# Slots of matching offsets, one task for two blocks of dots, and a third conv pair behind the layer norm's mean

## The chip, the cores and the metric

The kernel runs on one core of one Trainium2 chip. The metric is the time of one execution on the device in microseconds (us), as a median over runs. The engines are named as in the profile: PE is TensorE, DVE is VectorE, ACT is ScalarE, POOL is GpSimd, SP is SyncE, which here only issues DMAs.

## What is computed

Two residual layers on one sequence of 1024 tokens with 1024 channels, in float32. Each layer has a token mixer and a gated feed-forward part, each behind a root-mean-square norm whose result is shifted and scaled by vectors that come from a conditioning vector `c`. The stack ends with one more norm.

```
c_act = silu(c)
for i in range(2):
    mod = c_act @ ada_w[i] + ada_b[i]
    sh_m, sc_m, g_m, sh_f, sc_f, g_f = split(mod, 6)
    h = rms_norm(x, norm_mix_g[i]) * (1 + sc_m) + sh_m
    if i == 0:      # convolution module
        a, g = split(h @ w1 + b1, 2)
        u = a * sigmoid(g)
        u = causal_depthwise_conv(u, w_dw, width=31) + b_dw
        y = silu(layer_norm(u, ln_g, ln_b)) @ w2 + b2
    else:           # pooling mixer
        y = pooled_differences(h) @ w_grp * ls
    x = x + (1 + g_m) * y
    h = rms_norm(x, norm_ffn_g[i]) * (1 + sc_f) + sh_f
    x = x + (1 + g_f) * ((silu(h @ w_gate) * (h @ w_up)) @ w_down)
return rms_norm(x, final_g)
```

## The kernel before, in words

**Layout.** Channels lie on the 128 partitions, so a tensor of 1024 channels is 8 tiles (`KT`), and the 2816 channels inside the feed-forward part are 22 tiles (`NF`). The tokens are cut into two chunks of 512, A (`ch.i == 0`) and B (`ch.i == 1`). A product therefore multiplies a 128x128 weight block with a 128x512 operand.

**Three products for one.** Each float32 operand is split into a high part and a low part in the type float32r, and `products` (L423) issues three matmuls: weight high with operand high, weight high with operand low, weight low with operand high. A weight tile is loaded as 512 KB through SP (`raw`); ACT copies the high part and its negative, and a DMA from POOL adds the tile once more to the negative, which leaves the low part (`load_weight`, L408). Up to five weight tiles are held ahead (`W_BUFS`).

**Where the operands lie.** `slot_after` (L243) draws tiles of `ch.n + 2 - 2 * ch.i` values: 514 values, 2056 bytes, in chunk A and 512 values, 2048 bytes, in chunk B. `slot` (L239) hands out the last 512 values of such a tile. In these slots lie the high and low parts of the normed input (`hhi`, `hlo`), of the conv module's last operand (`vhi`, `vlo`), of the pooled differences (`mxhi`, `mxlo`), and of the conv input for the taps that TensorE takes (`uhi`, `ulo`). A second kind, `wslot` (L247), is 542 values, 2168 bytes, wide, eight per chunk: the gated conv input `u` with 30 values of history ahead of it, the normed input `hp` of the pooling mixer, and the high and low parts of the feed-forward's inner values (`ghi`, `glo`, L900).

**The order of the work.** The program is a list of units (L547) that are emitted one after the other. TensorE's order is the order of emission. Beside the units there are tasks (`Task`, L210, and `Taps`, L660) that give small steps to VectorE, GpSimd and ScalarE. `pace` (L187) is called every few products and lets tasks step as long as an estimated clock of the engine is less than 4 us ahead of the estimated clock of TensorE. `finish` (L199) emits all that is left of a task, with no regard to pauses. A task can ask for a pause in estimated time (`LOAD`: "load" and "next" 4.0, "slow" 18.0, "dots" 3.5 us).

**The convolution stage.** `conv_in` (L601) computes one tile of `a` and one of `g` of a chunk, a pair of 24 matmuls each, and `conv_glu` gates them into `u`. The 31 taps of a tile of A are then a `Taps` task: each tap is one operation on VectorE (accumulator in PSUM) or, with a helper multiplication on ScalarE, one addition on GpSimd. Tile 7 of A is taken by TensorE with all 31 taps, and tile 6 with eight (`PE_TAPS`, L46), as products with diagonal matrices (`pe_taps`, L636); a tap that reaches back by an odd number of tokens reads its operand one value off. When the taps of all eight tiles are there, `layer_norm_silu` (L739) sums the tiles, TensorE spreads the mean, VectorE centres, ScalarE squares, and so on up to `vhi` and `vlo`. Then `conv_out` (L780) multiplies them with `w2`, 192 matmuls, and adds up the squares for the next norm.

The units stand in this order: pairs 4 and 5 of A; pairs 6 and 7 of A and then of B; pairs 0, 1, 2 of B; the tap units of tiles 6 and 7; then the taps of A are finished; pairs 3 and 4 of B (`HOLD_LN = 2`), in whose course the mean comes; `conv_out` of A; pair 5 of B with the norm of the feed-forward part of A (`norm_a`); then the feed-forward part of A, during which VectorE and GpSimd do the taps and the layer norm of B.

**The dots.** Most of `mod` is computed on VectorE: `ada_dot` (L315) multiplies a 128x1024 tile of `ada_w`, 512 KB, with `c_act` and sums it. A block of `mod` (one of the six parts `j`) takes eight dots. `ada_task` (L324) makes a task of them; its tiles go through two buffers (`ADA_BUFS`) that all such tasks share, loaded by SP. Blocks 4 (the scale of the feed-forward norm) and 5 (the gate behind it) of layer 0 are two tasks that are put up ahead of `conv_out` of A; behind `conv_out` the unit at L1147 finishes that of block 4. Block 4 is needed by `norm_a`, block 5 by the first down products. The 48 dots of layer 1 are one task, put up at the start of the feed-forward part of A with pauses of 18 us; `ada_need` (L1099) forces what is missing in the third unit of B's feed-forward part.

**The feed-forward parts.** For each chunk and layer: `ffn_p1` computes one tile of gate and up, 24 matmuls each, `ffn_p2` the down products of two such tiles, 48 matmuls, six for each of the eight output tiles. They follow in the order A layer 0, B layer 0, A layer 1, B layer 1, with the mixers of layer 1 between.

Of the kernel before, what the change touches and what calls it, by code (L numbers as in the profile page):

```python
# [16 lines left out]
P = 128  # L17
# [8 lines left out]
WINDOWS = (2, 4, 8, 16)  # L26
PHALO = max(WINDOWS) - 1
EPS = 1e-6

# [85 lines left out]
def trunk(ctx, tc, xT, c, vec, ada, adan, w1f, w1, wdg, w2, wgu, wdn, wpl, out):  # L115
# [123 lines left out]
    def slot(ch, name, dt=F32R):  # L239

        return slot_after(ch, name, dt)[:, 2 - 2 * ch.i :]

    def slot_after(ch, name, dt=F32R):  # L243

        return slots.tile([P, ch.n + 2 - 2 * ch.i], dt, tag=f"s{ch.i}", name=nm(name))

    def wslot(ch, name, dt=F32):  # L247

        return slots.tile([P, ch.width], dt, tag=f"u{ch.i}", name=nm(name), bufs=KT)

# [324 lines left out]
    def conv_u(ch, p):  # L575
        u = st["u", ch.i, p] = wslot(ch, "u")
        if ch.i == 0:
            G_.memset(u[:, :HALO], 0.0)
        else:
            G_.tensor_copy(u[:, :HALO], uhalo[:, p, :])  # L580
        return u

    def conv_glu(ch, p, ba, bg):
# [3 lines left out]
        if ch.i == 0 and PE_TAPS.get(p) == CW:  # L587

            V_.scalar_tensor_tensor(ba, ba, V("conv_b1", p), sg, op0=ADD, op1=MUL)
            hi, lo = st["us", p] = [slot_after(A, name) for name in ("uhi", "ulo")]  # L590
            for part in (hi, lo):
                G_.memset(part[:, :2].bitcast(F32), 0.0)
            S_.copy(hi[:, 2:], ba)
            V_.tensor_tensor(lo[:, 2:], ba, hi[:, 2:].bitcast(F32), op=SUB)
            S_.copy(uhalo[:, p, :], ba[:, ch.n - HALO :])
            return
# [4 lines left out]
    def conv_in(*todo):  # L601

        def emit(take):
            got = {}
            for each in todo:
# [14 lines left out]
                conv_glu(ch, p, *b)  # L620
                if ch.i == 0 and 0 < PE_TAPS.get(p, 0) < CW:
                    split_u(p)
                if ch.i == 0 and PE_TAPS.get(p, 0) < CW:
                    T["taps", 0, p] = Taps(A, p, PE_TAPS.get(p, 0))
        tiles = list(dict.fromkeys(e[1] for e in todo if e))
        unit(emit, *[w1[p, i] for p in tiles for i in range(2)])

    def split_u(p):


        u = st["u", 0, p][:, HALO - 2 :]
        hi, lo = st["us", p] = [slot_after(A, name) for name in ("uhi", "ulo")]
        S_.copy(hi, u)
        either(A.n).tensor_tensor(lo, u, hi.bitcast(F32), op=SUB)

    def pe_taps(p):  # L636

        groups = tap_groups(p)
        us = []
        for i, js in enumerate(groups):  # L640
            def emit(take, i=i, js=js):
# [3 lines left out]
                for q, j in enumerate(js):  # L645
                    o = (CW - 1 - j) // 2 * 2
                    i0 = 2 - (CW - 1 - j) % 2
                    products(b[:, o:], wt, q, [v[:, i0 : i0 + A.n - o] for v in st["us", p]], j == CW - 1, j == CW - PE_TAPS[p])
                    if q % 4 == 3:
                        pace()  # L650
                if i == len(groups) - 1:
                    if PE_TAPS[p] == CW:
                        S_.activation(st["u", 0, p][:, HALO:], b, AF.Identity, bias=V("conv_bdw", p))
# [6 lines left out]
    class Taps:  # L660
# [4 lines left out]

        def __init__(self, ch, p, others=0):
            self.ch, self.p, self.done, self.urgent = ch, p, False, False
            self.next, self.acc, self.part = 0, None, None

            self.end, self.awaits, self.other = CW - max(others, 1), others > 0, None  # L670
            tasks.append(self)

        def step(self, e):
# [4 lines left out]
            if self.done:  # L678
                return False
            if self.next < self.end:  # L680
                if e == "V" and self.acc is None and sum(isinstance(t, Taps) and t.acc is not None for t in tasks) >= 2:
                    return False
                if e == "G":
                    if self.acc is None and self.part is None and sum(isinstance(t, Taps) and t.part is not None for t in tasks) >= 2:
                        return False
                    if self.next >= self.end - 2:
                        return False
                j = self.next
                self.next += 1
                if e == "V":  # L690
# [18 lines left out]
            if e != "V" or self.awaits and self.other is None:  # L709
                return False  # L710
            d = u[:, HALO : HALO + n]
            if self.awaits:
                if self.part is not None:
                    V_.tensor_tensor(d, self.part, self.acc, op=ADD)
                else:
                    S_.copy(d, self.acc)
                V_.tensor_tensor(d, d, self.other, op=ADD)
            else:
                if self.part is not None:
                    V_.tensor_tensor(self.acc, self.part, self.acc, op=ADD)  # L720
                V_.scalar_tensor_tensor(d, d, w(CW - 1), self.acc, op0=MUL, op1=ADD)
            self.done = True
# [84 lines left out]
    def pool_h(ch, l):  # L807

        hp = st["hp", ch.i] = [wslot(ch, "hp") for _ in range(KT)]
        for k in range(KT):  # L810
# [62 lines left out]
    def ffn_p1(ch, l, f, pick, first):  # L873
        def emit(take):
# [385 lines left out]
```

## Time and profile before

| | us |
|---|---|
| runs, median of 3 | 1873.54 |
| lowest and highest | 1871.35, 1875.83 |
| the profiled execution | 1871.14 |
| its span, first to last instruction | 1869.4 |
| PE, DVE, ACT, POOL busy | 1826.0, 990.9, 968.0, 614.8 |

An execution of the profile has a start and an end of each instruction. A matmul of the profile lasts longer than the distance to the next one, since matmuls are pipelined; so the cost of a product is read from the time that a run of them takes, divided by their number. A row of the timeline has start and length in us, engine, line, operation, the tiles by name as out<-in, and in brackets the idle time of the engine before it and what ended that. Nearly all instructions have line 109 or 131, the helpers that issue them, so they are told apart by tile. The granted clock is 1.00 where TensorE runs at full speed and 0.50 where it is given half.

### The profile page before, as it was taken

The numbers are of one execution on the slowest core, as the hardware profiler recorded it, in microseconds if no ns is written. First come the engines' busy times: TensorE is split into PE (matmuls) and PEld (weight loads), VectorE is DVE, ScalarE is ACT, GpSimd is POOL, SyncE is SP. The second block draws the span as 40 slices with busy tenths as digits, with TensorE's granted clock in tenths as the row PEclk, the third lists the DMA queues.
The fourth block names the chain that finished last, engine by engine and source line by source line (L and its number), as shares of the span: only waits on it lengthen the run. The fifth ranks groups of instructions, "written<-read, shape, count | busy, mean of one in ns | idle before, by whom it ended". The sixth has DMA issues, their size and how long they took to land.

```text
span 1869.4 us, 21783 instructions
## 1 busy us (share of the span) xinstructions
PE 1826.0 (98%) x8085; PEld 1481.9 (79%) x8085; DVE 990.9 (53%) x1528; ACT 968.0 (52%) x1240; POOL 614.8 (33%) x662
## 2 busy tenths in 40 slices
PE   7999998999999999999999999999999999999997
PEld 5777776888888888877888888888888888888886
DVE  8899856988875235585622233734432233322225
ACT  3775665766656454454644445644534454444443
POOL 4587522877733211272111111511111111111111
PEclk9999998999999999999999999999999999999998
DMA  7958797888978987999887878778778879788782
GB/s 289 300 151 221 172 263 222 225 222 208 223 189 216 231 221 185 283 261 269 227 194 178 211 171 205 182 173 205 181 178 196 192 177 250 176 205 197 181 195 68
DMA packets 108285, 387.56 MB, mean 207 GB/s; under 512 B 11793, under 2 KB 13969, under 8 KB 108178
## 3 DMA queue, kind: packets, MB, share of 16 engines
q0 software_dynamic: 44208, 160.98, 47.2%
q1 hardware_dynamic: 62880, 224.13, 34.6%
q8 instruction: 64, 1.05, 0.2%
q10 hardware_dynamic: 1090, 1.05, 0.2%
q14 instruction: 43, 0.35, 0.1%
HBM read 381.92 MB, written 4.19 MB: 207 GB/s over the span
## 4 chain that ended last, share of the span: by engine, by line
PE 82%; DVE 10%; DMA 6%; issue 1%; ACT 1%; SPq 0%; POOL 0%; DVEq 0%
PE gate L131 24%; PE up L131 24%; PE dn L131 24%; DMA adaw<-in_ada_dram 5%; DVE ca L109 4%; PE y L131 4%; PE first L131 3%; DVE adaw L109 1%; DVE acc L109 1%; PE g L131 1%; PE a L131 1%; DVE x L109 1%; DVE t L109 1%; DMA adaw<-in_adan_dram 1%; DVE hlo L109 1%
## 5 line engine op out<-in xcount | busy, mean ns | idle before, releaser
L109 ACT CAST w<-raw 128x1024 fp32r<-128x1024 f32 x317 | 331.0, 1044 | 508.2 <-issue 303.8
L131 PE MATMUL gate<-hhi,w 128*128 128x512 f32 x1408 | 455.4, 393 | 2.3 <-DVE x L109 1.7
L131 PE MATMUL up<-hhi,w 128*128 128x512 f32 x1408 | 455.9, 393 | 0.0
L131 PE MATMUL dn<-ghi,w 128*128 128x512 f32 (+1 forms) x1440 | 445.7, 386 | 1.2 <-DMA w<-in_wdn_dram 1.2
L417 POOL DMA_DIRECT2D w<-in_wgu_dram x176 | 154.6, 878 | 779.0 <-ACT w L109 759.4
L109 ACT ACTIVATE w<-raw 128x1024 fp32r<-128x1024 f32 x307 | 323.9, 1055 | 0.0
L109 DVE SCALAR_TENSOR_TENSOR x<-dn,gains,x 128x512 f32<-128x512 f32 (+1 forms) x360 | 261.8, 735 | 115.8 <-PE dn L131 115.3
L109 DVE TENSOR_TENSOR t<-t,up 128x512 f32<-128x512 f32 x86 | 59.0, 686 | 495.0 <-PE up L131 474.8
L131 PEld LDWEIGHTS dn<-ghi,w 128*128 128x128 f32 x1440 | 267.9, 188 | 59.8 <-DMA w<-in_wdn_dram 1.6
L131 PEld LDWEIGHTS gate<-hhi,w 128*128 128x128 f32 x1408 | 264.8, 188 | 62.6 <-DVE x L109 2.5
L131 PEld LDWEIGHTS up<-hhi,w 128*128 128x128 f32 x1408 | 264.7, 188 | 59.2 <-DMA w<-in_wgu_dram 0.3
L131 PE MATMUL dn<-glo,w 128*128 128x512 f32 (+1 forms) x720 | 278.7, 387 | 0.0
L131 PE MATMUL gate<-hlo,w 128*128 128x512 f32 x704 | 276.7, 393 | 1.5 <-DVE hlo L109 1.5
L131 PE MATMUL up<-hlo,w 128*128 128x512 f32 x704 | 276.5, 393 | 0.0
L109 POOL TENSOR_TENSOR pa<-pa,pr 128x512 f32<-128x512 f32 x156 | 222.9, 1545 | 13.6 <-ACT pr L109 10.9
L109 DVE SCALAR_TENSOR_TENSOR ca<-u,vecs,ca 128x512 f32<-128x512 f32 x257 | 177.8, 745 | 0.5
L131 PEld LDWEIGHTS gate<-hlo,w 128*128 128x128 f32 x704 | 132.6, 188 | 31.5 <-DVE hlo L109 2.3
L131 PEld LDWEIGHTS dn<-glo,w 128*128 128x128 f32 x720 | 135.2, 188 | 28.1 <-issue 0.2
L131 PEld LDWEIGHTS up<-hlo,w 128*128 128x128 f32 x704 | 132.6, 188 | 29.2
L417 POOL DMA_DIRECT2D w<-in_wdn_dram x88 | 78.3, 890 | 228.4 <-ACT w L109 226.5
L109 DVE SCALAR_TENSOR_TENSOR adaw<-adaw,cact 128x1024 f32<-128x1024 f32 x80 | 118.9, 1488 | 65.1 <-DMA adaw<-in_ada_dram 65.0
L109 ACT ACTIVATE t<-gate 128x512 f32<-128x512 f32 x86 | 51.1, 594 | 157.4 <-PE gate L131 155.4
(145 smaller groups left out, 1776.7 us busy)
## 6 DMA issues: line engine op xcount, KB each, us to landing
raw<-in_wgu_dram SPq DMA_DIRECT2D x176, 512.0 KB, 7.5
w<-in_wgu_dram POOLq DMA_DIRECT2D x176, 512.0 KB, 8.1
raw<-in_wdn_dram SPq DMA_DIRECT2D x88, 512.0 KB, 5.3
w<-in_wdn_dram POOLq DMA_DIRECT2D x88, 512.0 KB, 9.4
adaw<-in_ada_dram SPq DMA_DIRECT2D x64, 512.0 KB, 7.6
raw<-in_w_dram SPq DMA_DIRECT2D x36, 512.0 KB, 6.4
w<-in_w_dram POOLq DMA_DIRECT2D x34, 512.0 KB, 8.5
adaw<-in_ada_dram SPq DMA_DIRECT2D x8, 1024.0 KB, 5.3
```

Of the source, the lines that this page charges most:

```text
L109: self.last = self.order(getattr(self.eng, name)(out, *args, **kw))
L131: last_mm[0] = nc.tensor.matmul(out, lhsT, rhs, start=start, stop=stop).ins.name
L417: order(nc.gpsimd.dma_start(low if len(src.shape) == 2 else low.rearrange("p (a b) -> p a b", a=src.shape[1]), src, accum_op=ADD))
```

## The change

Five edits:

1. **Slots.** `slot` is 512 values, 2048 bytes, for both chunks, with no offset. The wider slots come in pairs, one tile of 2 x 544 values (4352 bytes): `u` and `hp` of two neighbouring tiles share one, and the high and low parts of `g` lie in one, the low part 576 values, 2304 bytes, behind the start of the high one. The split input of tile 7 takes a pair of chunk B's.
2. **Taps.** Tile 6 gets 15 taps on TensorE in place of 8, the ones with an even number (28, 26 ... 0), all read from offset 0. The task keeps the others and the last one. The split of tile 6 is made behind pair 7 of A.
3. **Order.** `HOLD_LN` is 3: pairs 2, 3 and 4 of B stand behind the finish of A's taps, where before only pairs 3 and 4 did.
4. **Dots of layer 0.** Blocks 4 and 5 are one task with a first pause of 18 us and 4.0 us for the others, put up ahead of pair 2 of B. The unit behind `conv_out` steps this task until block 4 is there.
5. **Dots of layer 1.** Their task is put up three units later, ahead of the first down products of A, where the task of blocks 4 and 5 is finished.

The core of the diff:

```
+WSLOT = 544
...
-HOLD_LN = 2
-PE_TAPS = {6: 8, 7: CW}
+HOLD_LN = 3
+PE_TAPS = {6: 15, 7: CW}
...
-LOAD = {"load": 4.0, "slow": 18.0, "next": 4.0, "dots": 3.5}
+LOAD = {"load": 4.0, "slow": 18.0, "next": 4.0, "dots": 4.0}
...
-    todo = list(range(CW - 1, CW - 1 - PE_TAPS[p], -1))
+    todo = list(range(CW - 1, -1, -1) if n == CW else range(CW - 3, CW - 3 - 2 * n, -2))
...
     def slot(ch, name, dt=F32R):
-        return slot_after(ch, name, dt)[:, 2 - 2 * ch.i :]
+        return slots.tile([P, ch.n], dt, tag=f"s{ch.i}", name=nm(name))
...
+    def wpair(ch, name, dt=F32):
+        return slots.tile([P, 2, WSLOT], dt, tag=f"u{ch.i}", name=nm(name), bufs=KT // 2)
...
+    def gslots(ch):
+        pair = wpair(ch, "g", F32R)
+        return pair[:, 0, : ch.n], pair[:, 1, WSLOT - ch.n :]
...
-    def ada_task(l, js, pause=None):
+    def ada_task(l, js, pause=None, first=None):
...
-                yield pause or ("next" if lax[0] else "slow")
+                yield first if first and i == 0 else pause or ("next" if lax[0] else "slow")
...
-            hi, lo = st["us", p] = [slot_after(A, name) for name in ("uhi", "ulo")]
+            pair = wpair(B, "us", F32R)
+            hi, lo = st["us", p] = [pair[:, i, : ch.width] for i in range(2)]
...
-                if ch.i == 0 and 0 < PE_TAPS.get(p, 0) < CW:
-                    split_u(p)
...
+                if ch.i == 0 and p == KT - 1:
+                    for q in PE_TAPS:
+                        if PE_TAPS[q] < CW:
+                            split_u(q)
...
-            hi, lo = st["g", ch.i, f] = [wslot(ch, name, F32R)[:, : ch.n] for name in ("ghi", "glo")]
+            hi, lo = st["g", ch.i, f] = gslots(ch)
...
+    unit(lambda take: T.__setitem__("ada_f", ada_task(0, (4, 5), "dots", "slow")))
     for p in rest[len(rest) - HOLD - HOLD_LN : len(rest) - HOLD]:
         conv_in((B, p))
     need("ln_a")
-    unit(lambda take: [T.__setitem__(("ada", 0, j), ada_task(0, (j,), "dots")) for j in (5, 4)])
     sq_a = Squares(A)
     conv_out(A, sq_a, lambda take: [now(columns_done(*g)) for g in held_back])
-    unit(lambda take: finish(T["ada", 0, 4]))
+    def scale_done(take):
+        forced[0] = True
+        while (0, 4) not in ada_done:
+            step(T["ada_f"], "V")
+        forced[0] = False
+    unit(scale_done)
...
-    unit(lambda take: T.__setitem__(("ada", 1), ada_task(1, range(6))))
     taps(B, *range(KT))
...
     for i, (e, ws) in enumerate(fa):
+        if i == GROUP + 1:
+            unit(lambda take: finish(T["ada_f"]))
+            unit(lambda take: T.__setitem__(("ada", 1), ada_task(1, range(6))))
```

More of the change, by code (lines that the diff above doesn't have):

```diff
@@ L239, in slot, with wslot @@
     def slot(ch, name, dt=F32R):
-        return slot_after(ch, name, dt)[:, 2 - 2 * ch.i :]
[L243 to L249, printed above, removed]
+        return slots.tile([P, ch.n], dt, tag=f"s{ch.i}", name=nm(name))
+    def wpair(ch, name, dt=F32):
+        return slots.tile([P, 2, WSLOT], dt, tag=f"u{ch.i}", name=nm(name), bufs=KT // 2)
+    def wslot(ch, name, p):
+        if st.get((name, "pair", ch.i), (None,))[0] != p // 2:
+            st[name, "pair", ch.i] = p // 2, wpair(ch, name)
+        return st[name, "pair", ch.i][1][:, p % 2, : ch.width]
+    def gslots(ch):
+        pair = wpair(ch, "g", F32R)
+        return pair[:, 0, : ch.n], pair[:, 1, WSLOT - ch.n :]
     def bank(name):
@@ L575, in conv_u @@
     def conv_u(ch, p):
[L576 removed]
+        u = st["u", ch.i, p] = wslot(ch, "u", p)
         if ch.i == 0:
@@ L628, in split_u @@
     def split_u(p):
-        u = st["u", 0, p][:, HALO - 2 :]
-        hi, lo = st["us", p] = [slot_after(A, name) for name in ("uhi", "ulo")]
+        u = st["u", 0, p][:, HALO - 2 : HALO - 2 + A.n]
+        hi, lo = st["us", p] = [slot(A, name) for name in ("uhi", "ulo")]
         S_.copy(hi, u)
@@ L645, in emit @@
                 for q, j in enumerate(js):
-                    o = (CW - 1 - j) // 2 * 2
-                    i0 = 2 - (CW - 1 - j) % 2
-                    products(b[:, o:], wt, q, [v[:, i0 : i0 + A.n - o] for v in st["us", p]], j == CW - 1, j == CW - PE_TAPS[p])
+                    full = PE_TAPS[p] == CW
+                    o = (CW - 1 - j) // 2 * 2 if full else CW - 3 - j
+                    c = j + o if full else 0
+                    products(b[:, o:], wt, q, [v[:, c : c + A.n - o] for v in st["us", p]], j == groups[0][0], j == groups[-1][-1])
                     if q % 4 == 3:
@@ L660, in trunk, with __init__ @@
     class Taps:
-        def __init__(self, ch, p, others=0):
+        def __init__(self, ch, p):
             self.ch, self.p, self.done, self.urgent = ch, p, False, False
-            self.next, self.acc, self.part = 0, None, None
-            self.end, self.awaits, self.other = CW - max(others, 1), others > 0, None
+            self.acc, self.part, self.other = None, None, None
+            others = tap_groups(p) if ch.i == 0 and p in PE_TAPS else []
+            self.todo, self.awaits = [j for j in range(CW - 1) if not any(j in js for js in others)], bool(others)
             tasks.append(self)
@@ L711, in step @@
             d = u[:, HALO : HALO + n]
+            if self.part is not None:
+                V_.tensor_tensor(self.acc, self.part, self.acc, op=ADD)
+            V_.scalar_tensor_tensor(d, d, w(CW - 1), self.acc, op0=MUL, op1=ADD)
             if self.awaits:
[L713 to L716, printed above, removed]
                 V_.tensor_tensor(d, d, self.other, op=ADD)
[L718 to L721, printed above, removed]
             self.done = True
@@ L807, in pool_h @@
     def pool_h(ch, l):
-        hp = st["hp", ch.i] = [wslot(ch, "hp") for _ in range(KT)]
+        hp = st["hp", ch.i] = [wslot(ch, "hp", k) for k in range(KT)]
         for k in range(KT):
```

18 lines of the change are left out of this document (9 added, 9 removed).

## The prediction

> **What bounds the kernel now.** I read the page first, then the chain that ended last, then the stretches between the stages, then TensorE's and VectorE's instructions in order of time around the widest holes.
>
> ```profile
> span 1869.4 us, 21783 instructions
> PE 1826.0 (98%) x8085; PEld 1481.9 (79%) x8085; DVE 990.9 (53%) x1528; ACT 968.0 (52%) x1240; POOL 614.8 (33%) x662
> L131 PE MATMUL gate<-hhi,w 128*128 128x512 f32 x1408 | 455.4, 393 | 2.3 <-DVE x L109 1.7
> L131 PE MATMUL dn<-ghi,w 128*128 128x512 f32 (+1 forms) x1440 | 445.7, 386 | 1.2 <-DMA w<-in_wdn_dram 1.2
> ```
>
> TensorE is busy for 98% of the span, so a gain needs cheaper products, or holes closed; only 43 us are holes. The same products do not cost the same in the two chunks. From the chain that ended last (start us, length us):
>
> ```profile
> 335.10 5.61 PE gate L131 x24
> 346.32 10.99 PE dn L131 x48
> 649.64 43.52 PE y L131 x192
> 854.10 5.44 PE gate L131 x24
> 875.97 5.49 PE gate L131 x24
> 886.90 11.22 PE y L131 x48
> ```
>
> At 335 chunk A is in the feed-forward part, at 854 chunk B: the same 24 products take 5.61 us in A and 5.44 us in B, with no idle time in either. Chunk B's operands lie in slots 2048 bytes apart; chunk A's lie 2056 bytes apart. The down products (10.99 per 48, or 5.50 per 24) read slots 2168 bytes apart in both chunks. Chunk B's conv output (649.64) runs at 5.44 per 24, so 226.7 ns each is what aligned slots give; A's mixer output (886.90) takes 5.61 per 24. I read this as: operands that follow each other at unlike offsets cost TensorE time.
>
> Now the stretches:
>
> ```profile
> 120.00:145.00 25.00, 25.00 (x130) 19.02 (x127) 25.00 (x26) 19.88 (x29) 24.64 (x29) 1.00 0.65 167
> 145.00:170.00 25.00, 24.81 (x129) 18.16 (x128) 25.00 (x33) 12.61 (x18) 14.37 (x14) 1.00 0.61 165
> 239.00:286.00 47.00, 45.92 (x193) 36.05 (x193) 24.81 (x39) 30.23 (x39) 11.98 (x12) 1.00 0.96 273
> 286.00:324.00 38.00, 28.77 (x115) 22.16 (x114) 26.86 (x51) 18.17 (x25) 9.29 (x13) 0.87 0.77 226
> 324.00:650.00 326.00, 326.00 (x1413) 264.48 (x1412) 234.88 (x333) 205.29 (x270) 189.96 (x172) 1.00 0.86 215
> 740.00:905.00 165.00, 162.16 (x716) 132.65 (x715) 108.38 (x161) 87.17 (x112) 66.89 (x93) 1.00 0.96 268
> ```
>
> Columns: length, then busy time of TensorE, its weight loads, VectorE, ScalarE, GpSimd, the granted clock, DMA share, GB/s. From 324 on TensorE has no hole to speak of. Before 217 VectorE is full as well (25.00 of 25.00): the taps of chunk A. The worst stretch is 286 to 324, with 9 us of holes and the clock at 0.87.
>
> **Alignment in the feed-forward parts.** The change makes the slots of both chunks 2048 bytes apart and puts each pair g in a tile of 4352 bytes, its low part 2304 bytes behind the high one; all of these are multiples of 256. Chunk A has 2 layers x 22 x 2 = 88 gate and up groups (1408 high products of gate, by 16 a group, are 88 for both chunks, so 44 for A, and as many for up). The first two stand in the norm stage below; 86 x (5.61 - 5.44) = 14.6 us. The down products are 43 groups of 48 (the last group, cut in halves, aside): 43 x (10.99 - 10.88) = 4.7 us, where 10.88 is 2 x 5.44. About ten of B's gate groups right behind down products take 5.49: 0.5 us. A's mixer output 11.22 - 10.88 = 0.3 us. Together **-20.1 us**. TensorE is the only bound there, so all of it counts; weights then have to come in A at the rate that B already takes. If the pair tiles don't bring the down products to 5.44, -15.4 remain; -21 is the other end, with all settling gone.
>
> SBUF — State Buffer, section Specifications (TRN2), in the Trainium skill, says that SBUF has lines of 16 bytes and that each crossing to a new line costs. By that a shifted operand of 512 values touches 129 lines for 128, an estimate of 0.8%, and the -20.1 would be about -5; the rows show 3.1% (5.61 to 5.44), so the measured size is used.
>
> **Up to the layer norm's mean.**
>
> ```profile
> L109 DVE SCALAR_TENSOR_TENSOR ca<-u,vecs,ca 128x512 f32<-128x512 f32 x123 | 85.1, 742 | 0.4
> L109 POOL TENSOR_TENSOR pa<-pa,pr 128x512 f32<-128x512 f32 x66 | 94.4, 1572 | 5.8 <-ACT pr L109 4.8
> L417 POOL DMA_DIRECT2D w<-in_w_dram x17 | 17.3, 1020 | 27.0 <-ACT w L109 25.9 <-POOL pa L109 1.0
> 216.88 1.12 PE L131 MATMUL mean<-acc,ones 128*128 128x512 f32 x2 [1.66 <-DVE acc L109]
> ```
>
> The first three rows are of the stretch 60 to 217. TensorE reaches the mean at 215.2 and waits 1.66 us for VectorE. Seven taps of tile 6 leave VectorE and GpSimd: one costs 0.69 us (85.1/123) on the one, 1.57 on the other, so 7 shared are 7/(1/0.69 + 1/1.57) = 3.4 us. One conv pair's gating goes behind the mean (-0.75), and GpSimd starts two weight loads less and one more (1.0 each), worth about 0.4 us of VectorE. The mean is ready **4.5 us earlier**, at 212.4; bounds 0 and -5.6 (all seven off VectorE).
>
> TensorE comes earlier still:
>
> ```profile
> 218.01 2.77 PE a L131 x12
> 220.78 5.44 PE g L131 x24
> 228.94 0.79 PE var L131 x8
> 232.56 0.89 PE rstd L131 x8
> ```
>
> A pair is 2 x 5.44 = 10.9 us. One pair leaves (-10.9), 21 tap products come (21 x 0.229 = +4.8), and about 375 products of A before this point get cheaper by 0.17/24 (-2.7): 215.2 - 8.8 = 206.4. So the wait grows from 1.66 to about 6 us. Up to here VectorE is the bound, and alignment and fewer products buy nothing. Queued behind the wait on TensorE are the rest of pair 2, pairs 3 and 4 and all that follows.
>
> What such a wait does to the clock:
>
> ```profile
> 178.20:181.60 3.40, 3.40 (x9) 2.62 (x9) 3.40 (x7) 2.25 (x5) 3.09 (x3) 0.50 1.05 289
> 297.00:304.50 7.50, 7.20 (x20) 5.51 (x20) 3.15 (x12) 0.81 (x1) 0.87 (x1) 0.50 1.02 292
> 297.06 1.87 PE L131 MATMUL var<-ones,acc 128*128 128x1 f32 x8 [5.47 <-DVE acc L109]
> ```
>
> Behind the 5.47 us wait at 297 the clock is 0.50 for 7.5 us (3.75 us lost); behind a shorter one at 177 for 3.4 us (1.7 lost). I take **+2.7**, bounds 0 and 3.75. TensorE: Matmul & The Clock Gate, Part 1 in the Trainium skill, speaks against this side of the change: an idle window of about 3.4 us halves the clock, and a busy one lifts it again, which by that figure is 1.7 us lost in place of 2.7; the 7.5 us at 0.50 above show that it can be more.
>
> **Between the mean and chunk A's conv output.** One more pair stands there: 10.9 and a little settling, **+11.0 us**. Today the first conv output products wait for the norm (47.00 us for 193 products, against 43.52 for 192 in B). With 11 us more cover that wait goes and the slots are aligned: **-3.5 us**.
>
> **The dots.** This is where the stretch 286 to 324 loses its time:
>
> ```profile
> L109 DVE SCALAR_TENSOR_TENSOR adaw<-adaw,cact x17: 1210/1226/2133, 244.5 to 332.5; 128x1024 f32<-128x1024 f32 x17
>   DMA adaw<-in_ada_dram: 26.3, 12
> DMA to landing us min/median/max: 3.4/6.1/12.3
> 293.36 1.22 DVE L109 SCALAR_TENSOR_TENSOR adaw<-adaw,cact 128x1024 f32<-128x1024 f32 x1 [1.81 <-DMA adaw<-in_ada_dram]
> 295.17 1.22 DVE L109 SCALAR_TENSOR_TENSOR adaw<-adaw,cact 128x1024 f32<-128x1024 f32 x1
> 296.31 0.69 DVE L109 TENSOR_TENSOR acc<-acc,t 128x512 f32<-128x512 f32 x1
> 310.37 0.51 PE L131 MATMUL gate<-hhi,w 128*128 128x512 f32 x1 [0.59 <-ACT hhi L109]
> 312.26 0.50 PE L131 MATMUL gate<-hlo,w 128*128 128x512 f32 x1 [1.38 <-DVE hlo L109]
> 323.89 5.61 PE gate L131 x24
> ```
>
> Two tasks with 3.5 us each share two buffers, so a dot is due every 1.75 us while a load takes 6.1 us to land; VectorE, which works in order, stands 26.3 us at them, the squares' sum behind them ends at 297, and variance and gate wait. After the change one task has a dot every 4 us (at the places where the planner is asked, about 5) and two buffers, so 8 us or more to land; it starts a first dot 18 us behind pair 2, some 35 us earlier than now. The eight of the scale then end within the conv output, and the forced step finds nothing to force. Queued behind the dots on VectorE are now the norm's own steps, which have 11 us of cover. On SP the loads stand ahead of weights; five buffered tiles of 5.4 us cover that.
>
> The stretch from 286 to 323.9 without waits is 96 products x 0.2267 + 0.79 + 0.89 = 23.4 us; I keep the gate's two waits (2.0) and 1.2 for one dot of the last eight that gets in the way: 26.6 against 37.9, **-11.3 us**. Bounds: -14.5 (no wait kept) and -4 (four of the last eight still wait as now).
>
> **Layer 1's dots start 33 us later.**
>
> ```profile
> 332.53 2.13 DVE L109 SCALAR_TENSOR_TENSOR adaw<-adaw,cact 128x1024 f32<-128x1024 f32 x1
> L109 DVE SCALAR_TENSOR_TENSOR adaw<-adaw,cact x29: 1204/1224/3491, 720.8 to 898.5; 128x1024 f32<-128x1024 f32 x29
>   DMA adaw<-in_ada_dram: 38.2, 14
> DMA to landing us min/median/max: 3.2/8.6/15.7
> ```
>
> 48 dots less 29 leave 19 between 332.5 and 720.8, one per 20.4 us. Three units of 11 us are then about two dots, which fall to the forced step in B's third unit. VectorE is held about 5.5 us by each (1.2 and half a landing); six banks of 1.36 us give TensorE 8 us of cover. **+1 us**, bounds 0 and 6.
>
> The later split of tile 6, the extra tap weights (1 MB under 5 us of products) and the split of tile 7 in a slot of chunk B (free again before pair 4 asks for it) I cost at nothing: each lies beside full TensorE work before the mean, where 6 us are idle.
>
> **Sum.** -20.1 - 4.5 + 11.0 + 2.7 - 3.5 - 11.3 + 1 = -24.7 us. The profiled execution took 1871.1 us (span 1869.4 and 1.7 around it), so 1846.4; the median of the runs, 1873.5, lies 2.4 above it: **1848.8 us**.
>
> **Rivals.**
> - The pair tiles don't line up: their distances are multiples of 256 but not of 512, and no row shows that case. The down products stay at 10.99: 1853.5; at A's 11.22 (43 x 0.23 dearer than that), 1863.4. Chance 0.10.
> - The dots still hold the norm: the last eight take the place of the first, since they stand in the same queue. -4 for -11.3: 1856. Chance 0.12. For it: DMA share is 0.96 from 239 to 286. Against: twice the time to land.
> - The wait at the mean is cheap (VectorE gets all seven taps off, no half clock, no waits at the gate: -1.1, -2.7 and -2.0): 1843. Chance 0.12.
> - The slots are not what makes A slow. Each shifted operand costs one line more in 128, and the rest of the 0.17 us belongs to chunk A in another way: -5 for -20.1, 1864; with nothing at all 1869. The rule on lines in SBUF — State Buffer of the Trainium skill (Specifications (TRN2)) would give the first. Against: A's conv output is slow and B's fast as well, with quite other neighbours. Chance 0.04.
> - Slower than before: the late layer 1. If not two but eight dots are forced in B's third unit, VectorE stands 8 x 5.5 = 44 us, the banks cover 8, and 36 us less the 1 already counted make 1883.8. It decides from seven dots on. Against: the count of two. Chance 0.03.
>
> **How the numbers follow.** The forecast has 0.59. A measurement of this kernel tells about 0.2%, 3.7 us, from no change. Faster by more than that are the forecast and the first three rivals: 0.93; the fourth, whose end at 1869 lies close to the bound, I count as within it, 0.04; slower 0.03. The range leaves out the fourth and the last rival and the worse end of the first, and takes the bounds of the single terms, which won't all fall on one side: 1841 to 1860.
>
> **What would show it.** Right: A's gate groups at 5.44, down groups at 10.88; a wait of 5 to 8 us before the mean and a clock of 0.5 behind it; no wait at the conv output; dots that wait a few us in all and a variance without wait; 286 to 324 shortened to under 30. Wrong: 5.6 in A, or a stretch before the feed-forward part that is no shorter than now.

## The result, and the profile after

The changed kernel takes **1844.03 us** (median of 4 runs, 1841.25 to 1849.92), the kernel before 1872.44 us in the runs beside it (median of 4, 1870.04 to 1875.83). The ratio is 0.985, with a 95% interval of 0.982 to 0.988: 28 us are gone, 24.7 were forecast. The profiled execution took 1849.92 us, the longest of the four, with a span of 1848.1 us.

The page of after, the rows that answer to those of before:

```profile
span 1848.1 us, 21822 instructions
PE 1805.3 (98%) x8106; PEld 1483.8 (80%) x8106; DVE 985.4 (53%) x1522; ACT 971.0 (53%) x1244; POOL 622.3 (34%) x662
L135 PE MATMUL gate<-hhi,w 128*128 128x512 f32 x1408 | 451.5, 390 | 1.9 <-DVE x L113 1.9
L135 PE MATMUL dn<-g,w 128*128 128x512 f32 (+1 forms) x2160 | 490.5, 386 | 0.7 <-DVE t L113 0.7
```

TensorE has 21 instructions more (the tap products of tile 6) and is busy for 20.7 us less. The chain that ended last, chunk A's conv output and its first feed-forward groups (start us, length us):

```profile
246.99 43.52 PE y L135 x192
...
317.71 5.45 PE gate L135 x24
323.17 5.44 PE up L135 x24
...
339.49 10.88 PE dn L135 x48
```

A's groups of 24 now take 5.44 us, the down groups 10.88, the conv output 43.52: the price that only chunk B's gate, up and conv output had before. The stretches in which the conv output and the norm lie:

```profile
239.00:286.00 47.00, 47.00 (x209) 38.94 (x208) 25.66 (x39) 30.77 (x42) 16.61 (x16) 1.00 0.95 265
286.00:324.00 38.00, 35.28 (x161) 28.44 (x161) 30.56 (x52) 26.38 (x35) 17.83 (x15) 1.00 0.81 229
```

Of the 9.2 us of holes between 286 and 324, 2.7 are left, and the granted clock is 1.00 where it was 0.87. VectorE's dots around them, by the view of their tile `adaw` (200 to 345 us):

```profile
L113 DVE SCALAR_TENSOR_TENSOR adaw<-adaw,cact x16: 1212/1219/4660, 238.5 to 333.3; 128x1024 f32<-128x1024 f32 x16
  DMA adaw<-in_ada_dram: 3.7, 3
DMA to landing us min/median/max: 3.2/7.3/12.0
```

VectorE waits 3.7 us for the dots' weights, not 26.3; a load takes as long to land as before (median 7.3 us; the same view of before, 200 to 345, has 7.4), but is given twice the time. TensorE's timeline shows what stayed, and where this execution lost time that is no part of the change:

```profile
24.37 0.79 PE L135 MATMUL first<-hhi,w 128*128 128x512 f32 x1 [2.58 <-ACT hhi L113]
216.81 1.10 PE L135 MATMUL mean<-acc,ones 128*128 128x512 f32 x2 [2.61 <-DVE acc L113]
304.01 0.50 PE L135 MATMUL gate<-hlo,w 128*128 128x512 f32 x1 [0.58 <-DVE hlo L113]
312.80 0.50 PE L135 MATMUL gate<-hlo,w 128*128 128x512 f32 x1 [0.31 <-DVE hlo L113]
316.29 0.50 PE L135 MATMUL gate<-hlo,w 128*128 128x512 f32 x1 [1.83 <-DVE hlo L113]
```

The variance and the reciprocal root have no wait any more; the gate's small waits stayed, as forecast. The first product began at 24.37 us, against 20.10 in before and 19.5 to 19.9 in every experiment below; it is the start-up of this one execution. The rest is read best as a table of stretches between the same products of TensorE, in us. The four columns on the right are experiments, told below.

| stretch | before | after | slots_only | two_dot_tasks | denser_layer1 | two_pairs_behind |
|---|---|---|---|---|---|---|
| start of the span to the first product | 20.10 | 24.37 | 19.67 | 19.75 | 19.78 | 19.54 |
| to the mean | 196.78 | 192.44 | 196.75 | 192.51 | 192.05 | 193.91 |
| to A's conv output | 21.88 | 30.01 | 23.53 | 30.01 | 30.00 | 26.42 |
| A's conv output | 47.20 | 43.52 | 46.39 | 43.52 | 43.52 | 43.52 |
| to the first gate product of A | 24.42 | 12.71 | 27.65 | 24.23 | 12.81 | 12.71 |
| that first unit | 13.36 | 14.50 | 12.84 | 13.01 | 14.46 | 14.47 |
| to B's conv output | 325.75 | 318.28 | 318.27 | 318.46 | 319.89 | 319.87 |
| B's conv output | 43.52 | 43.52 | 43.52 | 43.52 | 43.52 | 43.52 |
| to B's feed-forward part | 35.17 | 34.48 | 34.47 | 34.47 | 34.47 | 34.47 |
| its first six units | 89.71 | 93.99 | 89.18 | 93.47 | 88.87 | 93.06 |
| to A's layer 1 feed-forward part | 278.64 | 278.24 | 277.48 | 278.65 | 275.54 | 278.89 |
| that part | 382.30 | 373.57 | 373.57 | 373.57 | 373.57 | 373.57 |
| B's, to its last down product | 374.73 | 373.53 | 373.53 | 373.53 | 373.52 | 373.53 |

The last row ends at the last down product. Without the start-up, after is 25.5 us shorter than before: 24.7 by the rows of this table, and 0.8 in what follows the last down product.

Of the rows behind A's first unit one is worse: B's first six feed-forward units, where layer 1's dots are due. The stretch 690 to 900 of VectorE, and TensorE's two longest waits in it, with the window around the first:

```profile
L113 DVE SCALAR_TENSOR_TENSOR adaw<-adaw,cact x31: 1207/1224/2061, 706.6 to 888.4; 128x1024 f32<-128x1024 f32 x31
  DMA adaw<-in_ada_dram: 54.0, 12
```

```profile
784.77 1.26 PE L135 MATMUL rstd<-ident,col 128*128 128x128 f32 x8 [2.56 <-DVE col L113]
832.22 0.50 PE L135 MATMUL gate<-hhi,w 128*128 128x512 f32 x1 [1.86 <-DVE x L113]
```

```profile
781.00:793.00 12.00, 9.44 (x39) 7.52 (x38) 6.80 (x22) 3.22 (x5) 2.85 (x3) 0.86 1.05 293
```

VectorE stands 54.0 us at the dots' loads here, 38.2 before. What that does to TensorE is seen in VectorE's own timeline, ahead of the wait at 784 (between the two rows lie other dots, with at most 2.10 us of wait):

```profile
752.10 1.23 DVE L113 SCALAR_TENSOR_TENSOR adaw<-adaw,cact 128x1024 f32<-128x1024 f32 x1 [9.31 <-DMA adaw<-in_ada_dram]
780.17 1.23 DVE L113 SCALAR_TENSOR_TENSOR adaw<-adaw,cact 128x1024 f32<-128x1024 f32 x1 [7.71 <-DMA adaw<-in_ada_dram]
```

One dot keeps VectorE for 9.31 + 1.23 us, another for 7.71 + 1.23; the norm's column, queued behind the second, comes 2.56 us too late for TensorE, and the window's 0.86 over 12 us is 3.4 us at half clock besides. The wait at 832 has no such dot ahead of it, and before has it too, at the same products, shorter and with the clock at 1.00 behind it:

```profile
842.92 0.50 PE L131 MATMUL gate<-hhi,w 128*128 128x512 f32 x1 [1.38 <-DVE x L109]
```

### The profile page after: what moved, and what is told of

It reads as the page before. It is cut to its first block, busy times and chain, and to the rows that moved or that the text cites. A ratio compares the mean times of both kernels' runs of the same rounds, so it can differ in the third digit from the quotient of the medians.

```text
span 1848.1 us, 21822 instructions
## 1 busy us (share of the span) xinstructions
PE 1805.3 (98%) x8106; PEld 1483.8 (80%) x8106; DVE 985.4 (53%) x1522; ACT 971.0 (53%) x1244; POOL 622.3 (34%) x662
## 4 chain that ended last, share of the span: by engine, by line
PE 84%; DVE 10%; DMA 4%; issue 1%; ACT 0%; SPq 0%; DVEq 0%
PE gate L135 24%; PE up L135 24%; PE dn L135 24%; PE y L135 6%; DVE ca L113 4%; DMA adaw<-in_ada_dram 3%; PE first L135 2%; PE a L135 2%; PE g L135 2%; DVE acc L113 1%; DVE adaw L113 1%; DVE t L113 1%; DVE hlo L113 1%; DVE x L113 1%; DMA adaw<-in_adan_dram 1%
## 5 line engine op out<-in xcount | busy, mean ns | idle before, releaser
L135 PE MATMUL dn<-g,w 128*128 128x512 f32 (+1 forms) x2160 | 490.5, 386 | 0.7 <-DVE t L113 0.7
L135 PEld LDWEIGHTS dn<-g,w 128*128 128x128 f32 x2160 | 399.7, 189 | 82.5 <-DVE t L113 1.5
L135 PE MATMUL up<-hhi,w 128*128 128x512 f32 x1408 | 451.0, 390 | 0.0
L113 POOL TENSOR_TENSOR pa<-pa,pr 128x512 f32<-128x512 f32 x158 | 227.2, 1546 | 18.5 <-ACT pr L113 15.8
L113 DVE SCALAR_TENSOR_TENSOR ca<-u,vecs,ca 128x512 f32<-128x512 f32 x247 | 171.2, 746 | 0.2
L113 ACT ACTIVATE pr<-u,vecs 128x512 f32<-128x512 f32 x158 | 106.7, 714 | 27.4 <-DVE u L113 9.5
L113 DVE TENSOR_TENSOR g<-t,g 128x512 fp32r<-128x512 f32 x66 | 55.0, 833 | 62.5 <-ACT g L113 62.5
```

The costliest lines, as they stand in the source:

```text
L113: self.last = self.order(getattr(self.eng, name)(out, *args, **kw))
L135: last_mm[0] = nc.tensor.matmul(out, lhsT, rhs, start=start, stop=stop).ins.name
```

## The experiments

They ask four things: what makes a product dear; what the slots are worth alone; what the one task for two blocks is worth; and what layer 1's late dots cost, and the third pair. Each is an edit of the changed kernel. Theory 1 is the prediction's: moving operands that follow each other at unlike offsets cost time. Theory 2: what counts is how a moving operand lies to the weight tile.

In the built kernels' memory maps, by address modulo 256 bytes, the weight tiles lie at 64 in before and after alike. In before, chunk B's slots lie at 64 as well; chunk A's are 2080 bytes apart, not 2056, since each tile is rounded up to a multiple of 32, and are read at 72, 104, 136 and so on, never at 64; the pieces of `g` are 2176 bytes apart, at 64 and 192 in turn. In after everything lies at 64 but the input of tile 7's taps. Both theories fit both kernels.

### What makes a product dear: four offsets

**alike_off_8**: all of chunk A's slots, and `g` in both chunks, 8 bytes off the weights' class, but alike (four weight tiles held ahead in place of five, for room).

```
-        return slots.tile([P, ch.n], dt, tag=f"s{ch.i}", ...)
+        return slots.tile([P, ch.n + 64 * (1 - ch.i)], ...)[:, 2 * (1 - ch.i) :][:, : ch.n]
-        return pair[:, 0, : ch.n], pair[:, 1, WSLOT - ch.n :]
+        return pair[:, 0, 2 : 2 + ch.n], pair[:, 1, 2 : 2 + ch.n]      # WSLOT = 576
```

> All slots of chunk A lie 2304 bytes (9 x 256) apart and are read from byte 8; the high and low parts of g lie 2304 bytes apart and are read from byte 8 as well. So all operands of A's products start 8 bytes off, and alike. Four weight tiles are held ahead in place of five, for room. Theory 'alike': products pay only when consecutive operands start at unlike distances, so A's gate groups stay at 5.44 us per 24 and the down groups at 10.88 per 48. Rival 'own start': an operand that starts off a line pays by itself, so A's gate groups are at 5.6 us or more and the down groups at about 11.2.

**slots_2080, slots_2112, slots_2176**: chunk A's slots 2080, 2112 and 2176 bytes apart, and the low part of `g` 2176, 2240 and 2208 bytes behind the high one (for the last one four weight tiles).

```
+        return slots.tile([P, ch.n + 8 * (1 - ch.i)], ...)[:, : ch.n]    # 8, 16, 32
+        return pair[:, 0, : ch.n], pair[:, 1, : ch.n]                    # from 0, 16, 8
```

> Chunk A's slots lie 2080 bytes apart with no offset, so all start at multiples of 32 but in eight classes of 256; the low part of g lies 2176 bytes behind the high one (half a multiple of 256 off). Theory 'alike': A's gate groups go back to about 5.6 us per 24 and the down groups to 10.99 per 48, the time near 1862 us. Rival 'own start' (16-byte lines): every operand starts at a line, so 5.44 and 10.88 stay, 1844 us.

> Chunk A's slots lie 2112 bytes apart with no offset, all at multiples of 64, in four classes of 256; the low part of g lies 2240 bytes behind the high one (192 off a multiple of 256). Theory 'alike' with 256: A's gate groups between 5.5 and 5.6 us per 24 and the down groups about 10.99 per 48. Rival: what counts is the distance within 64 bytes, which is alike here, so 5.44 and 10.88 stay.

> Chunk A's slots lie 2176 bytes apart with no offset, so high parts are alike and low parts half a multiple of 256 away from them; the low part of g lies 2208 bytes behind the high one (160 off a multiple of 256). Four weight tiles are held ahead in place of five, for room. Theory 'alike' with 256: A's gate groups at 5.50 us per 24, as the down groups had in the kernel before, and the down groups about 10.99 per 48. Rival: the distance within 128 bytes counts, so A's gate groups stay at 5.44 and only the down groups change.

One execution each, beside 1870.86 us for before on the same chip: 1899.0, 1868.1, 1859.3 and 1887.7 us. The chains, at the same place in A's feed-forward part, first of alike_off_8:

```profile
402.92 5.60 PE gate L135 x24
...
414.12 11.20 PE dn L135 x48
```

of slots_2080:

```profile
404.42 11.19 PE dn L135 x48
415.62 5.56 PE gate L135 x24
```

of slots_2112:

```profile
401.63 10.98 PE dn L135 x48
412.61 5.53 PE gate L135 x24
```

and of slots_2176:

```profile
410.39 11.09 PE dn L135 x48
421.48 5.54 PE gate L135 x24
```

In all four, chunk B's gate and up groups stay at 5.44, or at 5.46 to 5.49 right behind a down group. In alike_off_8 the operands that follow each other lie alike, and still the full price is paid, on the down groups of both chunks too. That speaks against theory 1. The other three show that it is no matter of lines of 16 bytes either: distances that are multiples of 32, 64 and 128 bytes pay as well, with 5.53 to 5.59 (the lines of SBUF — State Buffer, section Specifications (TRN2), in the Trainium skill, would be crossed no oftener there than at 2048). With four weight tiles and dearer products the times are no measure of one cause; the group lengths are.

### Which of the two is moved

128 bytes are put in front of the slots and the weight tiles (**all_moved**), of the weight tiles alone (**weights_moved**) or of the slots alone (**slots_moved**, with 128 more ahead of the weights, so that they lie 256 on). What lies behind the weight tiles moves along.

```
+    shift   = cst.tile([P, 32], F32, name="shift")                # all_moved
+    shift_w = wts.tile([P, 32], F32, tag="shift", ..., bufs=1)    # weights_moved, slots_moved
+    shift_s = slots.tile([P, 32], F32, tag="shift", ..., bufs=1)  # slots_moved
```

> The changed kernel with 128 bytes put ahead of everything, so that slots and weight tiles all start 192 past a multiple of 256 in place of 64: alike to each other as before, but elsewhere. Theory 1, consecutive moving operands have to be alike: gate groups stay at 5.44 us and down groups at 10.88. Theory 2, moving operand and weights have to be alike: the same. Theory 3, the place itself counts: both are slower, 5.5 to 5.6 and 11.0 to 11.2.

> The changed kernel with the weight tiles moved by 128 bytes and the slots where they were: all moving operands are alike, all weights are alike, and the two differ by 128. Theory 1, consecutive moving operands: 5.44 and 10.88 stay. Theory 2, moving operand against weights: all groups of both chunks are slower, 5.5 to 5.6 and 11.0 to 11.2. Theory 3, the place of the moving operand itself: 5.44 and 10.88 stay.

> The changed kernel with the slots moved by 128 bytes and the weight tiles where they were. Theory 1, consecutive moving operands: 5.44 and 10.88 stay. Theory 2, moving operand against weights: all groups of both chunks are slower, 5.5 to 5.6 and 11.0 to 11.2. Theory 3, the place of the moving operand itself: the same slowness as by theory 2.

One execution each, beside 1869.43 us: 1841.5, 1880.4 and 1882.1 us. The chain of all_moved, with B's conv output as the last row:

```profile
595.04 10.88 PE dn L135 x48
605.92 5.44 PE gate L135 x24
...
627.68 43.52 PE y L135 x192
```

of weights_moved:

```profile
605.57 11.16 PE dn L135 x48
616.73 5.57 PE gate L135 x24
...
639.03 44.62 PE y L135 x192
```

of slots_moved:

```profile
606.35 11.20 PE dn L135 x48
617.55 5.60 PE gate L135 x24
...
639.95 44.80 PE y L135 x192
```

The slots are the same tiles, alike among themselves, in all three. Moved together with the weights they cost nothing, so the place as such does not count; moved by themselves they cost 2.4 to 2.9%, and so do the weights moved by themselves. **Theory 2 holds and theory 1 falls**: the distance between the moving operand and the weight tile, modulo 256 bytes, decides whether there is a price. 128 bytes between them pay; steps of 256 that are no multiple of 512 (the pair tiles, 4352 apart) are free. Where all operands are off, the price is 0.13 to 0.17 us per 24 products of 5.44 us.

Left open is what sets its size where only some operands are off. In before, by the maps, half of the down groups have the low part of `g` off the weights (one product of three, as at 346.32), the other half the high part (two of three, as in the row below); both cost the same:

```profile
413.12 11.00 PE dn L131 x48
```

And A's down groups of slots_2080 take 11.19 and B's 10.99, from pair tiles that lie alike in classes. One of B's, begun at 792 behind a wait, runs as A's do, with 230 to 236 ns from product to product, where the next ones have 226 to 234. So what ran just before seems to count too; no run here isolates it.

### The slots alone

**slots_only**: two pairs behind the mean, eight taps of tile 6 on TensorE (even-numbered ones, read as in the change), two tasks of dots and layer 1's dots as in before; otherwise only the slots and pair tiles of the change.

```
-HOLD_LN = 3
+HOLD_LN = 2
-PE_TAPS = {6: 15, 7: CW}
+PE_TAPS = {6: 8, 7: CW}
-    ... ada_task(0, (4, 5), "dots", "slow")            # "dots": 4.0
+    ... [... ada_task(0, (j,), "dots") for j in (5, 4)]  # "dots": 3.5, ahead of conv_out of A
```

> The changed kernel with everything but the slots undone: two pairs behind the mean, eight taps of tile 6 on TensorE (even-numbered ones), two tasks of dots ahead of the conv output at 3.5 us, layer 1's dots put up at the start of the feed-forward part. Theory: the slots are worth about 20 us in the feed-forward parts and 1 us in chunk A's conv output, nothing before the mean, and the waits at the norm stay (some 12 us between 286 and 324): 1852 us. Rival, the schedule brings the gain: no faster than 1868 us.

1850.13 us, ratio to before (1870.24) 0.989 (0.987 to 0.992): some 20 of the 28 us. By the table, the parts behind the first unit of A lose 7.48 + 0.70 + 0.53 + 1.16 + 8.73 + 1.20 = 19.8 us. The norm's waits are still there, in TensorE's timeline of slots_only:

```profile
298.29 1.87 PE L135 MATMUL var<-ones,acc 128*128 128x1 f32 x8 [6.35 <-DVE acc L113]
308.72 2.05 PE L135 MATMUL rstd<-ident,col 128*128 128x128 f32 x8 [3.29 <-DVE col L113]
```

### Two tasks of dots

**two_dot_tasks**: the changed kernel with the dots of blocks 4 and 5 as two tasks ahead of A's conv output, as in before.

```
-    ... ada_task(0, (4, 5), "dots", "slow")            # "dots": 4.0, behind pair 2
-    unit(scale_done)
+    ... [... ada_task(0, (j,), "dots") for j in (5, 4)]  # "dots": 3.5, ahead of conv_out of A
+    unit(lambda take: finish(T["ada", 0, 4]))
```

> The changed kernel with the dots of blocks 4 and 5 as two tasks again, put up ahead of the conv output at 3.5 us each. Theory: VectorE stands at the loads again and the variance comes late, so the stretch from the end of A's conv output to the feed-forward part grows from 12.7 to 22 us or more: some 10 us slower than the changed kernel, 1854 us. Rival: the third pair gives the dots enough time in any case, no difference to the changed kernel, 1844 us.

1855.38 us, 0.992 (0.990 to 0.995), so 11 us slower than the change. The timeline of two_dot_tasks has before's wait again, in spite of the longer cover ahead of the conv output:

```profile
298.47 1.87 PE L135 MATMUL var<-ones,acc 128*128 128x1 f32 x8 [7.08 <-DVE acc L113]
```

The stretch to the first gate product goes from 12.71 to 24.23: the single task is worth 11.5 us there, 10.0 with the unit behind it (13.01 for 14.50). The edit changes the number of tasks, their start and their pause at once; which of them does it was not tried.

### Layer 1's dots, denser

**denser_layer1**: one dot of layer 1 per 15.5 us of estimated time in place of 18; the first pause of the task before stays at 18.

```
-LOAD = {..., "slow": 18.0, ..., "dots": 4.0}
+LOAD = {..., "slow": 15.5, ..., "dots": 4.0, "first": 18.0}
-    ... ada_task(0, (4, 5), "dots", "slow")
+    ... ada_task(0, (4, 5), "dots", "first")
```

> The changed kernel with layer 1's dots 15.5 us apart in place of 18 (the first pause of blocks 4 and 5 stays 18). Theory: the 4 to 5 us lost in B's third to sixth feed-forward units come from the two or three dots that the later start leaves to the forced step; with three more done ahead that loss goes: 1840 us. Rival: they come from the 24 dots behind it and their loads, which are as many as before: 1844 us.

1836.03 us, 0.982 (0.979 to 0.984). VectorE's dots between 690 and 900 in denser_layer1:

```profile
L113 DVE SCALAR_TENSOR_TENSOR adaw<-adaw,cact x28: 1207/1219/2327, 703.3 to 869.3; 128x1024 f32<-128x1024 f32 x28
  DMA adaw<-in_ada_dram: 27.6, 8
```

Three dots fewer are left for this stretch, VectorE's waits are halved (27.6 for 54.0), and TensorE has one wait left between 700 and 900, 1.21 us for a weight tile at 845.59: its two stretches go from 93.99 to 88.87 and from 278.24 to 275.54. These 7.8 us are what the change lost by its late dots; the medians say 8.0, the ratios to the before of each round 6.4. The stretch to B's conv output is 1.6 us longer (319.89 for 318.28), but that is not the denser dots: two_pairs_behind has the same with the old pause. In both, a wait at the gate that the change has too (1.81 us at 311.36, 1.83 in after) was followed by 3.4 us at half clock, and in after it was not.

### The third pair

**two_pairs_behind**: two pairs of B behind the mean as in before, with a first pause of the dots of 7 us, since the mean comes sooner after they are put up.

```
-HOLD_LN = 3
+HOLD_LN = 2
-    ... ada_task(0, (4, 5), "dots", "slow")
+    ... ada_task(0, (4, 5), "dots", "first")     # "first": 7.0
```

> The changed kernel with two pairs behind the mean (the first pause of the dots 7 us in place of 18, so that they come at the same time). Theory: TensorE then reaches the mean some 8 us after VectorE is ready, so the mean comes 8 us later, the stretch from it to the conv output gets 8 us shorter, and 2 us of waits at the conv output come back: 2 us slower, 1846 us. Rival, the third pair costs its 8 us and brings nothing: 1836 us.

1843.96 us, 0.986 (0.984 to 0.988): no difference from the change's 1844.03. My expectation was off in its steps, as TensorE's timeline of two_pairs_behind shows:

```profile
213.44 1.10 PE L135 MATMUL mean<-acc,ones 128*128 128x512 f32 x2 [1.60 <-DVE acc L113]
230.67 1.16 PE L135 MATMUL rstd<-ident,col 128*128 128x128 f32 x8 [1.58 <-DVE col L113]
```

The mean is bound by VectorE here too and comes 1.5 us later from the first product; the reciprocal root waits 1.58; but no wait comes back at the conv output (43.52), and the stretch ahead of it is 3.6 us shorter. Of that, 1.6 goes again on the way to B's conv output, by the half clock told above. With 15 taps of tile 6 on TensorE, the third pair neither costs nor gains by the medians; by these stretches two pairs are 2 us the shorter, the clock aside.

**dense_two_pairs** joins the last two edits ("slow" 15.5, "first" 7.0, `HOLD_LN = 2`).

> The changed kernel with layer 1's dots 15.5 us apart and two pairs behind the mean. Theory: the two gains hold beside each other, 8 us for the dots and 0 to 2 us for the pairs, 1834 to 1836 us. Rival: the pairs' order matters once the dots are out of the way, and it ends off by more than 3 us from 1836.

1837.74 us, 0.983 (0.981 to 0.985), no better than denser_layer1. The best of the versions is the change with layer 1's dots at 15.5, 1836.0 us.

## Why the prediction was right, and where it was not

**The sum** was -24.7 us; the profiles show -25.5 without the start-up, the medians -28.4 (by the interval -22 to -33), so the change took 1844.0 us where 1848.8 was forecast. That the sum lies so close is in part luck: the way from the mean to the conv output came out 5.6 us better than forecast, layer 1's dots 4.6 us worse. Its terms:

- **Alignment, -20.1: right in size (-19.8 in slots_only), wrong in its reason.** The step that failed is "operands that follow each other at unlike offsets cost TensorE time". all_moved, weights_moved and slots_moved show that what counts is how the moving operands lie to the weights, not to each other: 10.88 us per down group with both moved by 128 bytes, 11.16 and 11.20 with one of them. The prices were read from groups that had exactly those offsets, so the sum came out all the same. That the change's slots came to lie in the weights' class was luck, since nothing in it was aimed at that: had it made all slots alike but 8 bytes off the weights, the prediction's reading would have forecast a gain and alike_off_8's groups would have come. And the down products were dear in both chunks because the two parts of `g` lay 128 bytes apart, so that one of them was off the weights: 10.99 for 10.88.
- **Up to the mean, -4.5:** -4.3. VectorE was the bound, as read.
- **Mean to conv output, +11.0 and +2.7:** +8.1, mis-sized. I set the extra pair wholly behind the mean, with a wait of 6 us and half a clock. The row at 216.81 shows a wait of 2.61 us: in the changed order the mean's products stand later in pair 2, so that part of the pair fills the wait. And the clock stayed whole behind it, which the change had no hand in: in slots_2080 a wait of 2.39 us at the same place (210.06) was followed by 3.4 us at 0.50.
- **A's conv output, -3.5:** -3.7. No wait, aligned.
- **Norm and first unit, -11.3:** -11.7 and +1.1, so -10.6. two_dot_tasks puts 10.0 of it on the single task, and shows that the dots, not the want of cover, held the variance. Two readings behind this term were off. The landing of 6.1 us counts earlier loads into the same tiles in; those of the stretch 200 to 345 took 7.4. And the first dot came at 238.5, 6 us earlier than before's 244.5 and not 35. What the traces show in its place is the order: block 4's eight dots are through at 279 and one dot lies between 290 and 309, where before has five and two_dot_tasks four.
- **Layer 1's dots, +1 (bounds 0 and 6):** mis-sized. Against slots_only, which has the same alignment and before's dots, the two stretches take 4.8 and 0.8 us more. I counted two forced dots at 5.5 us of VectorE, hidden by 8 us of banks. In fact single dots held VectorE for 10.5 and 8.9 us (9.31 and 7.71, and 1.23 each), longer than the banks reach, and the wait of 2.56 us that followed on TensorE cost 1.7 us more by the half clock behind it. The wait at 832 was 1.86 us for 1.38 in before, and here too half a clock came behind it. The end of 1883.8 that I gave this mechanism was far off, the mechanism was not; denser_layer1 undoes it.

**The rivals.** "Multiples of 256 but not of 512 don't line up" fell: the down groups take 10.88 from tiles 4352 bytes apart. The dots do not hold the norm any more. "The wait at the mean is cheap" came true for the clock and the wait (no half clock, 2.61 us), not for the gate's waits, which stayed; it gave 1843, close to what the layer 1 dots then left of it. Lines of 16 bytes fell, as the multiples of 32, 64 and 128 show.

What stays open: why the medians fell 3 us more than the one profiled pair (both lie inside the interval; the profiled execution was also the one with the lowest granted clock of the four, 0.994 against 0.995 to 0.997), and why the stretch up to the mean took 188.8 us in all_moved, 3.7 less than in after, though the two differ by 128 bytes alone; that stretch is VectorE's.

## What to carry to other kernels

Lay moving operands and weights at the same address modulo 256 bytes, and look at the addresses that the allocator gave, not at the tile sizes written in the code. Where an engine works in order and waits for loads, give each load as much time as it takes to land: one task with 8 us for each tile, and the block that is due first ahead, beat two that shared the same buffers and had 3.5. When a step is moved to a later start, count its whole supply up to the due time, and price a forced load by its longest landing, not by the median.

## What was not expected of the hardware

- A moving operand of 128x512 in float32r beside weights 128 bytes off modulo 256 took 5.57 to 5.60 us per 24 products against 5.44 (232 to 233 ns each against 226.7), the same with 8 bytes off (5.60). Moved together by 128 bytes, both kept 5.44.
- Short waits halved the clock. TensorE: Matmul & The Clock Gate, Part 1, in the Trainium skill, has an idle window of about 3.4 us ahead of it, and a window that runs freely. Here the waits of 2.56 us (at 784) and 1.86 us (at 832) were each followed by 3.4 us at half clock, while that of 2.61 us at the mean was not. The window 781 to 793 above and two more of after show it; the length at half clock is twice what is missing from 1.00 (8 x 0.21 is 1.7 us lost):

```profile
832.00:840.00 8.00, 7.78 (x27) 6.23 (x28) 8.00 (x13) 3.95 (x5) 3.20 (x5) 0.79 0.65 191
216.00:222.00 6.00, 5.19 (x21) 3.99 (x22) 4.10 (x7) 3.52 (x7) 4.05 (x4) 1.00 1.06 285
```

The record of the granted clock in the trace says more. The half-clock stretches of after begin at 99.61, 785.69 and 833.48 and last 3.41 us each, and they lie 201 and 14 times 3.413 us apart; so the clock changes at the bounds of windows of that length. The waits at 784 and 832 each lie in one window, the one at the mean is divided between two:

```profile
782.28:785.69 3.41, 0.92 (x9) 0.92 (x9) 2.84 (x11) 1.79 (x2) 0.00 (x0) 1.00 1.06 263
830.07:833.48 3.41, 1.55 (x7) 1.05 (x6) 3.41 (x4) 0.00 (x0) 2.15 (x2) 1.00 0.99 250
212.26:215.67 3.41, 1.95 (x9) 1.29 (x7) 3.13 (x5) 1.43 (x2) 0.38 (x1) 1.00 1.01 275
215.67:219.08 3.41, 2.27 (x8) 1.60 (x9) 1.41 (x3) 1.16 (x2) 1.32 (x2) 1.00 1.06 274
314.65:318.06 3.41, 1.77 (x8) 1.46 (x9) 3.41 (x4) 2.85 (x5) 3.33 (x3) 1.00 0.03 5
```

TensorE was busy for 0.92 and 1.55 us of the first two windows, and the clock was 0.50 in the next one; it was busy for 1.95, 2.27 and 1.77 us of the others, and the clock stayed at 1.00. The wait at the gate in denser_layer1 left 1.60 us of one window (309.28 to 312.69), and 0.50 followed. So in these rows a window that was idle for about half was enough, and a wait's price depends on where it falls. One case does not fit by its busy time: ahead of 99.61, with narrow products among the others (`ada`, 32 columns, and `var`, one), TensorE was idle for only 0.98 us of the window.
